# A fused hybrid decoder layer: two more groups of projections as Strassen's seven products, sums of x's blocks beside its normalisation, LayerNorm summed in the convolution

## The chip, the cores and the metric

The kernel runs on one core of one Trainium2 chip. The metric is the device time of one execution in microseconds. The kernel before takes 827.84 us, the median of 3 runs from 827.66 to 827.86.

The core has a matrix engine (TensorE, "PE" in the profile, with its weight loads apart as "PEld"), a vector engine (VectorE, "DVE"), a scalar engine (ScalarE, "ACT"), GpSimd ("POOL") and SyncE ("SP"), which here issues DMAs only. GpSimd and ScalarE issue a few DMAs too. Each engine takes its instructions in the order in which they were written into the program.

## The reference

x is one sequence of 512 tokens by 2048 channels, float32. The layer is:

```python
h = rms_norm(x, norm_g)
z = h @ w_in                                # 2048 x 7168
a_val, a_glu, a_gate, q, k, v, b_gate = jnp.split(z, SPLIT_POINTS, axis=-1)    # 1024 columns each
u = a_val * jax.nn.sigmoid(a_glu)
u = causal_depthwise_conv(u, conv_w, conv_b)                 # 31 taps
u = jax.nn.silu(layer_norm(u, conv_norm_g, conv_norm_b))     # over the 1024 channels of a token
u = u @ conv_pw_w + conv_pw_b                                # 1024 x 1024
y_a = u * jax.nn.silu(a_gate)
q, k = rms_norm of each of 16 heads
o = dilated_attention_mixture(q, k, v)
y_b = o * jax.nn.silu(b_gate)
return x + jnp.concatenate([y_a, y_b], axis=-1) @ w_out      # 2048 x 2048
```

## The kernel before

**Layout and exactness.** Everything stands transposed: channels on the 128 partitions, the 512 tokens along the free axis; x is 16 tiles of 128x512. Float32 products are made from halves: a number becomes a high half in float16 and a low half (the remainder) in float16, and `tri` (lines 366 to 368) multiplies high by high, high by low and low by high into the same bank of PSUM. So each product of a 128x128 block with 512 columns is three matmuls.

**Groups and units.** The weights are cut into groups of 512 output columns, in the order vg 0 to 3 (value and gate columns of the convolution branch together), q 0, k 0, v 0, bg 0, q 1, k 1, v 1, ag 0, ag 1, bg 1 (gates), pw 0, pw 1 (the pointwise projection, 1024 rows), wb 0 to 3 and wa 0 to 3 (the output projection in two parts). A unit is 4 k-blocks of a group: one load of 1 MB into a buffer `wf` (a ring of 6). vg 0 and vg 1, 8 units, run on raw x with another exact split (line 824). From vg 2 on a unit is 8 slots of 6 matmuls; a group of 16 k-blocks is 4 units, 192 matmuls of 512 columns. The weights of the next unit are split while the present one is multiplied: ScalarE makes the high half `wh` of 128x2048 (line 290), VectorE the low half `wl`, and then the buffer is free for the load of the unit six on. A float16 scale for each group comes from the sums of squares of its loaded weights (`measure`, line 182, four per group, then a small matmul, POOL and VectorE).

**The seven products.** The wa groups are already multiplied as 2x2 blocks by Strassen's scheme in Winograd's form: seven products of blocks instead of eight, with sums s1 to s4 of weight blocks and t1 to t4 of blocks of y. A part is a weight block of 128x1024 in two halves (`ws`, line 891 and the low beside it); its matmuls have 256 columns. The sums of weights are made in the load buffers, by DMAs of POOL's queue that accumulate, or by VectorE.

**Who orders the work.** There is no automatic scheduler. The program runs a clock of slots (`clock`); `after(n, fn)` puts a piece of work n slots later in a `calendar`; each slot first issues what is due, then `run_conv`, then the slot's 6 matmuls. `run_conv` fills VectorE with the convolution: each VectorE instruction is counted as 180 plus its free size (`Weighed`), a slot takes PACE = 1200 off the count, and convolution steps are issued while the count is below zero.

**The convolution and LayerNorm** (`conv`) are one generator. Each of 8 channel tiles takes 30 VectorE instructions on 128x512 (`cv<-u,cw,cv`) and one on ScalarE. Then LayerNorm: the 8 tiles are added into `lnacc`, a matmul with ones gives the mean (line 508), the tiles are centred and their squares added into `lnacc2`. `token_rsqrt` (line 344 on) takes the sum over channels with 4 small matmuls (line 350) into `lncol` (tokens on partitions), POOL takes the power -1/2 (line 160), four VectorE instructions make a diagonal, and a matmul with ones (line 360) spreads it to a row on all partitions, which ScalarE copies to `lnrow` (line 361). Each tile is multiplied by `lnrow` on VectorE, ScalarE applies Silu, and `split16` makes the two float16 halves of the tile `u` for the groups pw, both halves on VectorE. The projection's first unit is not written into the program before all 8 tiles are.

**Attention** runs in pairs of heads, 8 pairs, each beside 32 slots of projections: scores (line 663), maxima on VectorE, exponentials on ScalarE, halves `hl` of the normalised weights (for pairs 0 to 3 the high half on ScalarE, for pairs 4 to 7 on VectorE; the low half on VectorE), transposes by DMA, values (line 706).

```python
def run_conv():
    V.load = min(max(V.load - PACE, -PACE), 4 * PACE)
    wait[0] -= 1
    while (V.load < 0 or wait[1]) and wait[0] <= 0:
        n = next(convolution, 1)
        if n:
            wait[0] = n
```

## Time and profile before

| of the profiled execution | |
|---|---|
| its time, and its span | 827.54 us, 825.7 us |
| PE busy | 821.4 us, 99% |
| PEld busy | 458.9 us, 56% |
| DVE busy | 657.7 us, 80% |
| ACT busy | 502.4 us, 61% |
| POOL busy | 110.9 us, 13% |
| granted TensorE clock | 9 tenths of full speed or more in all 40 slices |
| PE waited for others | 1.2 us |
| DMA | 116.10 MB, mean 141 GB/s |

The span is the time from the first to the last instruction that the profiler saw; the execution's own time also has what lies around it. Busy time is the time in which an engine had an instruction running. [...] A row of a group reads: line, engine, operation, out<-in by the program's names, shapes, count, then busy us and mean ns of one, then the engine's idle time before it and what ended it. A row of a timeline reads: start, duration, engine, line, operation. The columns of the other views are told where they are shown.

### The profile page before, as it was taken

The numbers are of one execution on the slowest core, as the hardware profiler recorded it, in microseconds if no ns is written. First come the engines' busy times: TensorE is split into PE (matmuls) and PEld (weight loads), VectorE is DVE, ScalarE is ACT, GpSimd is POOL, SyncE is SP. The second block draws the span as 40 slices with busy tenths as digits, with TensorE's granted clock in tenths as the row PEclk, the third lists the DMA queues.
The fourth block names the chain that finished last, engine by engine and source line by source line (L and its number), as shares of the span: only waits on it lengthen the run. The fifth ranks groups of instructions, "written<-read, shape, count | busy, mean of one in ns | idle before, by whom it ended". The sixth has DMA issues, their size and how long they took to land.

```text
span 825.7 us, 12385 instructions
## 1 busy us (share of the span) xinstructions
PE 821.4 (99%) x4839; PEld 458.9 (56%) x4839; DVE 657.7 (80%) x1110; ACT 502.4 (61%) x683; POOL 110.9 (13%) x139
## 2 busy tenths in 40 slices
PE   9999999999999999999999999999999999999998
PEld 6887644444444444444444444444444444688887
DVE  6758889888888988878787978556765898988985
ACT  6666654353654446767674846766675758765741
POOL 0000010101413100002203101000010002413420
PEclk9999999999999999999999999999999999999999
DMA  9832232323344432626363753445252467579852
GB/s 334 331 123 102 102 105 100 109 95 108 110 128 124 136 111 103 165 103 165 84 177 93 184 132 106 135 109 159 86 132 103 136 207 252 106 176 266 160 100 67
DMA packets 88858, 116.10 MB, mean 141 GB/s; under 512 B 62176, under 2 KB 74208, under 8 KB 79584
## 3 DMA queue, kind: packets, MB, share of 16 engines
q1 hardware_dynamic: 80544, 107.37, 41.7%
q0 software_dynamic: 7968, 7.87, 6.7%
q8 instruction: 38, 0.62, 0.3%
q14 instruction: 20, 0.16, 0.1%
q10 hardware_dynamic: 288, 0.07, 0.0%
HBM read 88.56 MB, written 4.19 MB: 112 GB/s over the span
## 4 chain that ended last, share of the span: by engine, by line
PE 99%; DMA 0%; ACT 0%; DVE 0%; issue 0%; ACTq 0%
PE ps_l L366 26%; PE ps_l L368 26%; PE ps_l L367 26%; PE ps_l L824 11%; PE ps_s L367 2%; PE ps_s L366 2%; PE ps_s L368 2%; PE ps_s L663 2%; PE ps_o L706 2%; DMA wf<-w_dram 0%; PE ps_s L360 0%; PE ps_s L350 0%; PE ps_s L508 0%; ACT hh L322 0%; DVE res L72 0%; ACT wr L276 0%
## 5 line engine op out<-in xcount | busy, mean ns | idle before, releaser
L290 ACT ACTIVATE wh<-wf,ws 128x2048 f16<-128x2048 f32 x56 | 111.9, 1998 | 143.4 <-PE ps_l L367 137.4
L72 DVE SCALAR_TENSOR_TENSOR cv<-u,cw,cv 128x511 f32<-128x511 f32 (+14 forms) x240 | 160.9, 728 | 0.0
L72 DVE SCALAR_TENSOR_TENSOR wl<-wf,ws,wh 128x2048 f16<-128x2048 f32 x57 | 133.9, 2349 | 31.5 <-ACT wh L290 30.8
L366 PE MATMUL ps_l<-x,wh 128*128 128x512 f16 x384 | 145.6, 379 | 0.0
L366 PE MATMUL ps_l<-wh,x 128*128 128x512 f16 x384 | 145.6, 379 | 0.0
L368 PE MATMUL ps_l<-wh,x 128*128 128x512 f16 x384 | 145.5, 379 | 0.0
L367 PE MATMUL ps_l<-wl,x 128*128 128x512 f16 x384 | 145.5, 379 | 0.0
L368 PE MATMUL ps_l<-x,wl 128*128 128x512 f16 x384 | 145.5, 379 | 0.0
L367 PE MATMUL ps_l<-x,wh 128*128 128x512 f16 x384 | 145.5, 379 | 0.0
L182 ACT ACTIVATE junk<-wf 128x2048 bf16<-128x2048 f32 x68 | 129.1, 1899 | 2.4 <-DMA wf<-w_dram 2.1
L366 PEld LDWEIGHTS <-wh 128*128 128x128 f16 x544 | 53.2, 98 | 63.0 <-issue 3.9
L368 PEld LDWEIGHTS <-wl 128*128 128x128 f16 x544 | 53.2, 98 | 60.8
L367 PEld LDWEIGHTS <-wh 128*128 128x128 f16 x544 | 53.2, 98 | 58.1 <-issue 0.7
L196 POOL TENSOR_SCALAR ws<-ws 128x1 f32<-128x1 f32 x22 | 11.0, 499 | 401.3 <-DVE ws L72 401.3
L366 PEld LDWEIGHTS <-x 128*128 128x128 f16 x384 | 37.6, 98 | 46.5 <-issue 1.9
L368 PEld LDWEIGHTS <-x 128*128 128x128 f16 x384 | 37.6, 98 | 45.2
L367 PEld LDWEIGHTS <-x 128*128 128x128 f16 x384 | 37.6, 98 | 43.9
L891 ACT ACTIVATE ws<-wf,ws 128x1024 f16<-128x1024 f32 x28 | 32.0, 1144 | 29.3 <-DVE ws L72 6.3
L824 PE MATMUL ps_l<-xr,wr 128*128 128x512 f32 x192 | 48.2, 399 | 0.0
L824 PEld LDWEIGHTS ps_l<-xr,wr 128*128 128x128 f32 x192 | 36.1, 188 | 9.1 <-issue 0.5
L675 ACT ACTIVATE sx<-sx,st,sc 128x128 f32<-128x128 f32 (+1 forms) x64 | 40.9, 640 | 0.1
L72 DVE CUSTOM_DVE_ANT_0 sx<-ps_s,tab 128x512 f32<-128x512 f32 (+3 forms) x64 | 27.6, 487 | 16.5 <-PE ps_s L663 16.5
(213 smaller groups left out, 1394.6 us busy)
## 6 DMA issues: line engine op xcount, KB each, us to landing
wf<-w_dram SPq DMA_DIRECT2D x72, 1024.0 KB, 4.9
wf<-wf POOLq DMA_DIRECT2D x12, 512.0 KB, 5.9
x<-xt_dram SPq DMA_DIRECT2D x16, 256.0 KB, 6.9
res<-xt_dram SPq DMA_DIRECT2D x8, 512.0 KB, 6.8
out_dram<-res SPq DMA_DIRECT2D x15, 256.0 KB, 2.3
wf<-w_dram SPq DMA_DIRECT2D x7, 512.0 KB, 7.2
wf<-wf POOLq DMA_DIRECT2D x6, 256.0 KB, 6.2
wf<-w_dram SPq DMA_DIRECT2D x2, 256.0 KB, 3.3
```

Of the source, the lines that this page charges most:

```text
L72: return getattr(self.engine, name)(out, src, *args, **kw)
L182: A.activation(junk[:, :n], src, AF.Square, scale=scale, accum_out=acc)
L196: G.tensor_scalar(scale, scale, 1e-30, 2.0 ** (-2 * top), op0=OP.max, op1=OP.mult)
L290: A.activation(parts[i][0], raw[i], AF.Copy, scale=wscale[units[i][3:]][0])
L366: T.matmul(ps, ah, bh, start=first, stop=False)
L367: T.matmul(ps, ah, bl, start=False, stop=False)
L368: T.matmul(ps, al, bh, start=False, stop=last)
L663: T.matmul(ps[i, a], qs[hf, q][rows, p4, i * P:w], ks[hf, k][rows, p4, :w], start=n == 0, stop=n == 2)
L675: A.activation(xi, xi, AF.Exp, scale=sc, bias=neg[a][:, i:i + 1], accum_out=total[a][:, i:i + 1])
L706: T.matmul(po[rows, i * P:(i + 1) * P], vs[hf][j // 2][:, j % 2, 2 * p4 + a, vp * DH:(vp + 1) * DH], got["t", a][:, pp * (ALL // P) + FROM ...
L824: T.matmul(banks[group, m], wt[:, a, m * P:(m + 1) * P], xk[b], start=k == 0 and a == b == 0, stop=k == KC - 1 and a == 1)
L891: A.activation(t[:, 0], block(name), AF.Copy, scale=wscale["wa", g][0])
```

## The change

1. **vg 3 and v 0 as seven products.** A new function `input_products` does for these two groups what the wa groups do: 28 steps of 12 matmuls with 256 columns, 336 in a group. 14 parts of 128x1024 take the place of 4 splits of 128x2048. Each part's high half is on ScalarE, ordered 5 steps ahead of its matmuls, the low half on VectorE 4 steps ahead. Of the sums of weights, s2, s3 and s4 are accumulating DMAs of POOL's queue (two of each in a group), s1 is on VectorE. The products are combined on VectorE and ScalarE in tiles `cb`.
2. **Sums of x's blocks.** The right operands t1 to t4 are made for all 8 pairs of k-blocks by `sum_x`, from slot 58 on, one pair every 5 slots: four subtractions or additions on 128x256, two copies to float16 on ScalarE, two remainders on VectorE, into tiles `tx`. The normalised x (`xn`) is kept in slots for that.
3. **LayerNorm's sum** over the 8 tiles is made as the tiles are finished, all but the last two.
4. **LayerNorm's row** no longer goes through the diagonal and the matmul: POOL's queue writes `lncol` to memory (`by_token`) and reads it back spread over the partitions.
5. **Shorter order after it.** Waits for a given slot are dropped; product, Silu and split of a tile follow each 2 slots instead of 3; the first half in `split16`, and the high half of attention pairs 4 to 7, go from VectorE to ScalarE. The projection's units are written once the tiles they need are there, not all 8.
6. **Numbers.** The ring of load buffers has 8, `SLOTS` 35, PACE 1220, and 1400 from the first attention pair on. Two scale constants change. The DMA descriptor scratch of the queues is 2048 instead of the default. q's and k's normalisation is moved to a function (`norm_qk`) with the same work, for q and k as they stand.

Over the whole program VectorE has 24 more instructions with a scalar and two tensors, 64 more of two tensors and 48 fewer of a scalar and a tensor; ScalarE 87 more activations; POOL 14 more DMAs; TensorE 287 more matmuls, of which the two groups are 2 x (336 - 192) = 288.

```diff
-RING = 6
+RING = 8
-SLOTS = 36
+SLOTS = 35
-PACE = 1200
+PACE = 1220
-V_SHIFT = 16
-G_SHIFT = 10
+V_SHIFT = 13
+G_SHIFT = 8
...
+SEVEN = (("vg", 3), ("v", 0))
+LAST_SEVEN = SEVEN[-1]
+BY_DMA = ("s2", "s3", "s4")
+SUM_FROM = 58
+SUM_STEP = 10
+PACE_2 = 1400
+MEASURE = 8
...
-        V.tensor_scalar(t[:, 0, :], src, scale, None, op0=OP.mult)
+        A.activation(t[:, 0, :], src, AF.Copy, scale=scale)
...
-        t = temp("xn")
+        t = xn[k] = slot("xn")
...
+    def sum_x(j):
+        k = j + 4 * (j // 4)
+        (b11, b12), (b21, b22) = ((t[:, :H], t[:, H:]) for t in (xn.pop(k), xn.pop(k + 4)))
+        t12, t34 = temp("xs"), temp("xs")
+        t1, t2, t3, t4 = t12[:, :H], t12[:, H:], t34[:, :H], t34[:, H:]
+        to = tx[j] = (wide if j < 4 else att).tile([P, 4, 2, H], F16, name="tx", tag="wide" if j < 4 else "att")
+        V.tensor_sub(t1, b11, b12)
+        V.tensor_sub(t3, b12, b22)
+        V.tensor_add(t2, b22, t1)
+        V.tensor_sub(t4, b21, t2)
+        both = lambda t: t.rearrange("p (n t) -> p n t", n=2)
+        def high():
+            for n, t in ((0, t12), (2, t34)):
+                A.activation(to[:, n:n + 2, 0], both(t), AF.Copy)
+        def low():
+            for n, t in ((0, t12), (2, t34)):
+                V.tensor_tensor(to[:, n:n + 2, 1], both(t), to[:, n:n + 2, 0], op=OP.subtract)
+        after(1, high)
+        after(2, low)
...
+        if n == C:
+            by_token = dram.tile([S], F32, name="by_token")
+            G.dma_start(by_token.rearrange("(t p) -> p t", p=P), c)
+            G.dma_start(row, by_token.partition_broadcast(P))
+            return
...
+            if i0 == 0:
+                acc = slot("lnacc")
+                V.tensor_add(acc, cv[0], cv[1])
+            elif i0 < 6:
+                for i in (i0, i0 + 1):
+                    V.tensor_add(acc, acc, cv[i])
+                    yield 0
         wait[1] = True
-        acc = temp("lnacc")
-        V.tensor_add(acc, cv[0], cv[1])
-        yield 0
-        for i in range(2, 8):
+        for i in (6, 7):
             V.tensor_add(acc, acc, cv[i])
-            yield 1
         yield 3
...
-        while clock[0] % 8 != 4 or any(0 <= clock[0] - n < 8 for n in at_pair.values()):
+        while any(0 <= clock[0] - n < 8 for n in at_pair.values()):
             yield 1
         c = small.tile([P, NT], F32, name="lncol")
         row = temp("lnrow")
         for _ in token_rsqrt(acc2, C, LN_EPS, c, row):
-            yield 2
-        yield 2
+            pass
+        yield 7
         for i in range(8 + 2):
             if i < 8:
                 V.tensor_mul(cv[i], cv[i], row)
             if 1 <= i < 8 + 1:
                 A.activation(cv[i - 1], cv[i - 1], AF.Silu, scale=lng[:, i - 1:i], bias=lnb[:, i - 1:i])
-            yield 2
+            yield 1
             if i >= 2:
                 u16[i - 2] = split16(cv.pop(i - 2), scales["u"][0], "u16")
...
-            if hf == 0:
-                A.activation(hi, xi, AF.Copy, scale=r)
-            else:
-                V.tensor_scalar(hi, xi, r, None, op0=OP.mult)
+            A.activation(hi, xi, AF.Copy, scale=r)
...
-        V.load = min(max(V.load - PACE, -PACE), 4 * PACE)
+        pace = PACE_2 if 0 < min(at_pair.values(), default=0) <= clock[0] else PACE
+        V.load = min(max(V.load - pace, -pace), 4 * pace)
...
+    def input_products(i0):
+        kind, g = group = units[i0][3:]
+        by_token = kind in ("q", "k", "v")
+        weights, bank, got, done, free = {}, {}, {}, set(), set()
+        e = {}
+        def block(name, pair):
+            b = PLACE.get(name, name)
+            return raw[i0 + 2 * pair + (b[2] == "2")][:, :, H * (b[1] == "2"):][:, :, :H]
+        def add(name, pair):
+            if name == "s1":
+                V.tensor_tensor(block("a11", pair), block("a22", pair), block("a11", pair), op=OP.subtract)
+            else:
+                x, to = SUMS[name]
+                if name in BY_DMA:
+                    nc.gpsimd.dma_start(block(to, pair), block(x, pair), accum_op=OP.add)
+                else:
+                    V.tensor_tensor(block(to, pair), block(to, pair), block(x, pair), op=OP.add)
+        def hi(name, pair):
+            t = weights[name, pair] = part_pool.tile([P, 2, KU, H], F16, name="ws", tag="part")
+            A.activation(t[:, 0], block(name, pair), AF.Copy, scale=wscale[group][0])
+        def lo(name, pair):
+            t = weights[name, pair]
+            V.scalar_tensor_tensor(t[:, 1], block(name, pair), wscale[group][0], t[:, 0], op0=OP.mult, op1=OP.subtract)
+            done.add((name, pair))
+            for j in range(4):
+                mine = ("s2", "s4") if j % 2 else ("s1", "s3")
+                if all((n, j // 2) in done for n in mine) and all(m in free for m in range(j)) and j not in free:
+                    free.add(j)
+                    raw.pop(i0 + j)
+                    load(i0 + j + RING)
+                    after(MEASURE, lambda j=j: measure(i0 + j + RING))
...
+        ORDER = (("p1", "a11", "b11"), ("u", "a22", "t4"), ("x", "a12", "b21"), ("p7", "s3", "t3"), ("p5", "s1", "t1"),
+                 ("p6", "s2", "t2"), ("z", "s4", "b22"))
+        def product(n, pair, m):
+            to, w, x = ORDER[n]
+            if (pair, m) == (0, 0):
+                bank[to] = lin_ps.tile([P, 2, H], F32, name="ps_l", tag="ps_l")
+            ps, ms = bank[to][:, m], slice(m * P, (m + 1) * P)
+            for k in range(KU):
+                t, xs = weights[w, pair], x_part(x, pair, k)
+                first, last_ = pair == m == k == 0, pair == m == 1 and k == KU - 1
+                if by_token:
+                    tri(ps, [x[:, ms] for x in xs], (t[:, 0, k], t[:, 1, k]), first, last_)
+                else:
+                    tri(ps, [t[:, j, k, ms] for j in range(2)], xs, first, last_)
...
+        plan = [(2, scales_of), (4, lambda: copy("p1")), (8, lambda: copy("u")), (12, first_block), (16, lambda: copy("p7")),
+                (25, joint), (26, fifth), (27, sixth), (29, final), (30, lambda: out("12"))]
+        plan += [(26 if kind == "v" else 13, lambda: out("11")), (27, lambda: out("22")), (28, lambda: out("21"))]
+        if group == LAST_SEVEN:
+            plan.append((24, tx.clear))
+        plan += [(n, lambda name=name, pair=pair: add(name, pair)) for n, name, pair in
+                 ((-8, "s3", 0), (-7, "s3", 1), (3, "s2", 0), (4, "s2", 1), (8, "s4", 0), (9, "s4", 1), (9, "s1", 0), (11, "s1", 1))]
+        for n, (_, name, _) in enumerate(ORDER):
+            for pair in range(2):
+                at = 4 * n + 2 * pair - 5 + ((n, pair) == (1, 0))
+                plan += [(at, lambda name=name, pair=pair: hi(name, pair)), (at + 1, lambda name=name, pair=pair: lo(name, pair))]
+                for m in range(2):
+                    def matmuls(n=n, pair=pair, m=m):
+                        product(n, pair, m)
+                    plan.append((4 * n + 2 * pair + m, matmuls))
+        return plan
...
-            for k in range(KC):
-                after(NORM_FROM + k * (70 - NORM_FROM) // KC, lambda k=k: norm_x(k))
+            for n in range(KC):
+                after(NORM_FROM + n * (70 - NORM_FROM) // KC, lambda k=n // 2 + 4 * (n // 8) + 4 * (n % 2): norm_x(k))
+            for j in range(8):
+                after(SUM_FROM + SUM_STEP * j // 2, lambda j=j: sum_x(j))
...
-        if kind == "pw" and i == of_group[group][0]:
-            while 7 not in u16:
+        if kind == "pw":
+            need = KU * units[i][2] + KU - 1
+            while need not in u16:
...
-    nc = bacc.Bacc("TRN2", target_bir_lowering=False, num_devices=1)
+    nc = bacc.Bacc("TRN2", target_bir_lowering=False, num_devices=1, dynamic_dma_scratch_size=2048)
```

The order of instructions at three places. First TensorE's, where vg 3 begins (operands `x` are the halves of the normalised x, `wh`, `wl` the halves of a unit's weights, `ws` those of a part). Before:

```order
L368 LDWEIGHTS wl
L368 MATMUL ps_l<-x_948,wl 128x512
L366 LDWEIGHTS wh
L366 MATMUL ps_l<-x_975,wh 128x512
L367 LDWEIGHTS wh
L367 MATMUL ps_l<-x_975,wh 128x512
```

and with the change:

```order
L411 LDWEIGHTS wh
L411 MATMUL ps_l<-x_1021,wh 128x512
L412 LDWEIGHTS wh
L412 MATMUL ps_l<-x_1021,wh 128x512
L413 LDWEIGHTS wl
L413 MATMUL ps_l<-x_1021,wl 128x512
L411 LDWEIGHTS ws
L411 MATMUL ps_l<-x_638,ws 128x256
L412 LDWEIGHTS ws
L412 MATMUL ps_l<-x_638,ws 128x256
```

Each matmul still has a weight load of its own; the columns are 256 where they were 512.

Second POOL's, around LayerNorm's row (`lncol` is a value for each token, tokens on partitions; `ws` and `esc` are group scales). Before:

```order
L160 TENSOR_TENSOR lncol_4784<-lncol_4784,half_115 128x4
L196 TENSOR_SCALAR ws_4831<-ws_4831 128x1
L160 TENSOR_TENSOR ws_4831<-ws_4831,half_115 128x1
L379 TENSOR_TENSOR esc_4941<-wi_4412,xinv_127 128x1
L196 TENSOR_SCALAR ws_4992<-ws_4992 128x1
```

and with the change:

```order
L169 TENSOR_TENSOR lncol<-lncol,half 128x4
L396 DMA by_token<-lncol 128x4x1
L397 DMA lnrow<-by_token 128x512
L205 TENSOR_SCALAR ws<-ws 128x1
L169 TENSOR_TENSOR ws<-ws,half 128x1
```

The two DMAs stand behind the power and ahead of the next group's scale. On TensorE there are 132 matmuls of 512 columns between the column sums (L390 with the change) and the first matmul of pw 0; before, the timeline has them 72 us apart.

Third VectorE's, from the first product with `lnrow` to the first low half of `u` (`hl` are attention's halves, `wl` a unit's low half, `ws` and `wi` scales). Before:

```order
L72 TENSOR_TENSOR cv<-cv,lnrow 128x512
L72 SCALAR_TENSOR_TENSOR hl<-sx,st_4663,hl 128x128
L72 SCALAR_TENSOR_TENSOR hl<-sx,st_4663,hl 128x256
L72 SCALAR_TENSOR_TENSOR hl<-sx,st_4663,hl 128x384
L72 SCALAR_TENSOR_TENSOR hl<-sx,st_4663,hl 128x512
L72 TENSOR_SCALAR ws<-ws 128x1
L72 RECIPROCAL wi<-ws 128x1
L72 TENSOR_TENSOR cv<-cv,lnrow 128x512 x2
L72 SCALAR_TENSOR_TENSOR wl<-wf,ws,wh 128x2048
L72 TENSOR_SCALAR u_4947<-cv,us 128x512
L72 SCALAR_TENSOR_TENSOR u_4947<-cv,us,u_4947 128x512
```

and with the change:

```order
L80 TENSOR_TENSOR cv<-cv,lnrow 128x512
L80 SCALAR_TENSOR_TENSOR hl<-sx,st_5552,hl 128x128
L80 SCALAR_TENSOR_TENSOR hl<-sx,st_5552,hl 128x256
L80 SCALAR_TENSOR_TENSOR wl<-wf,ws,wh 128x2048
L80 SCALAR_TENSOR_TENSOR hl<-sx,st_5552,hl 128x384
L80 SCALAR_TENSOR_TENSOR hl<-sx,st_5552,hl 128x512
L80 TENSOR_SCALAR ws<-ws 128x1
L80 RECIPROCAL wi<-ws 128x1
L80 TENSOR_TENSOR cv<-cv,lnrow 128x512 x2
L80 SCALAR_TENSOR_TENSOR hl<-sx,st_5553,hl 128x128
L80 SCALAR_TENSOR_TENSOR hl<-sx,st_5553,hl 128x256
L80 SCALAR_TENSOR_TENSOR u_5805<-cv,us,u_5805 128x512
```

The first half of `u` (`u<-cv,us` in two operands) is gone from VectorE and the low half follows the second and third product directly; the fourth low half of `u` is 26 rows after the first product, with two low halves of units, 8 of attention, two gates and five small instructions among them. With the change the first unit of pw 0 is written once the first four tiles are.

193 lines of the change are left out of this document (158 added, 35 removed).

## The prediction

> **What bounds the kernel now.** I read the page first, then who TensorE waited for, then its order of time. The page's busy time and its chain of waits:
> ```profile
> PE 821.4 (99%) x4839; PEld 458.9 (56%) x4839; DVE 657.7 (80%) x1110; ACT 502.4 (61%) x683; POOL 110.9 (13%) x139
> PE 99%; DMA 0%; ACT 0%; DVE 0%; issue 0%; ACTq 0%
> ```
> The waits of engine PE, all of them:
> ```profile
> PE ps_s L138 <- POOL wz L135: 1.0, 1, 1.0
> PE ps_l L824 <- ACT hh L322: 0.2, 1, 0.2
> ```
> The numbers of a waits row are the us waited, how often, and the longest. TensorE waits 1.2 us in 825.7, at the start. So the time is the number of matmuls by the spacing of their starts, at a granted clock of 1.00 (rows below), and a change counts by the matmuls that it takes away and by the waits that it puts in. A matmul's duration says nothing of that (0.38 us for one of 512 columns, which starts 0.216 us after the last). The spacing is read from TensorE's timeline; both stretches hold 30 matmuls, so 29 spacings:
> ```profile
> 699.71 0.38 PE L368 MATMUL ps_l<-y,wl 128*128 128x512 f16 x1
> ...
> 705.97 0.38 PE L367 MATMUL ps_l<-y,wh 128*128 128x512 f16 x1
> 741.74 0.27 PE L366 MATMUL ps_l<-y,ws 128*128 128x256 f16 x1
> ...
> 744.91 0.27 PE L368 MATMUL ps_l<-y,ws 128*128 128x256 f16 x1
> ```
> 512 columns: 6.26/29 = 0.2159 us. 256 columns: 3.17/29 = 0.1093 us, in the wa groups, which already run seven products with a weight load for each matmul.
>
> **The change, part by part.**
>
> *Matmuls of vg 3 and v 0.* Each group goes from 192 of 512 columns to 336 of 256: 192 x 0.2159 = 41.45 us becomes 336 x 0.1093 = 36.72 us, 4.73 us less; twice, 9.46 us.
>
> *LayerNorm's spreading matmul.* The diagonal goes, and with it one piece of the chain of waits (second row; the first, the column sums, stays):
> ```profile
> 549.38 0.79 PE ps_s L350 x8
> 555.37 0.86 PE ps_s L360 x2
> ```
> 0.86 us less. **Saved: 10.32 us.** All else of the change only counts if TensorE has to wait for it.
>
> *Preparing the weights.* A group's 4 splits of 128x2048 become 14 of 128x1024, two sums on VectorE and six accumulating DMAs on POOL. Rows of the groups:
> ```profile
> L891 ACT ACTIVATE ws<-wf,ws 128x1024 f16<-128x1024 f32 x28 | 32.0, 1144 | 29.3 <-DVE ws L72 6.3
> L72 DVE SCALAR_TENSOR_TENSOR ws<-wf,ws 128x1024 f16<-128x1024 f32 x28 | 35.7, 1279 | 2.4 <-ACT ws L891 2.3
> wf<-wf POOLq DMA_DIRECT2D x12, 512.0 KB, 5.9
> ```
> A part is due 5 steps after its first half is ordered; a step is 12 matmuls, 1.31 us. 1.14 + 1.28 = 2.4 us against 6.6: hidden by 4 us. The s3 sum is ordered 15 steps (19.7 us) ahead of its use, s2 12 steps, s4 11: each against 5.9 us, hidden, even with 8 us for the second of a pair. The s1 sum waits on VectorE for the s2 DMA, 6 steps (7.9 us) after it: behind it stand lows and convolution, and it is 2 us early. POOL's queue behind a waiting DMA holds only group scales that are due a group later.
>
> *VectorE as a whole.* Added: 8 sums of x's blocks, each 4 subtractions of 256 and 2 of 512 (20 us in all, estimated from 0.60 us for one of 512, row below); a group's 14 lows for 4, its sums and its recombination, about 14 us each. Nearly all of it displaces convolution, which fills the steps. The filling is read here, in the stretch of vg 2 (PE, PEld, DVE, ACT and POOL busy, then clock and DMA) and in the timeline just after it:
> ```profile
> 97.00:138.50 41.50, 41.50 (x194) 18.80 (x193) 35.80 (x48) 20.79 (x21) 3.45 (x3) 1.00 0.31 110
> 141.17 2.34 DVE L72 SCALAR_TENSOR_TENSOR wl<-wf,ws,wh 128x2048 f16<-128x2048 f32 x1
> 143.43 7.15 DVE L72 SCALAR_TENSOR_TENSOR cv<-u,cw,cv 128x495 f32<-128x495 f32 x11
> 150.67 2.35 DVE L72 SCALAR_TENSOR_TENSOR wl<-wf,ws,wh 128x2048 f16<-128x2048 f32 x1
> ```
> One low and 11 taps are 2228 + 11 x 675 = 9650 units of the pacing, 8 x 1200, and took 9.4 us from low to low (141.17 to 150.67 is 9.50); a unit is 48 x 0.2159 = 10.4. At 1220 a step has 1.19 us of VectorE work in 1.30 (1.31 in seven products): still under. At 1400, once attention runs, it has 1.37 us. A step is longer there by the attention's own matmuls; from the first scores of one pair to those of the next, 32 steps:
> ```profile
> 306.84 0.61 PE L663 MATMUL ps_s<-k,q 64*128 64x512 f16 x4
> 352.16 0.82 PE L663 MATMUL ps_s<-k,q 64*128 64x512 f16 x5
> ```
> 45.32/32 = 1.42 us. It fits narrowly; a burst (the k group's evacuation ahead of v 0) can make a first part late by one low, 1.28 us. Three groups start behind such bursts: 0 to 3.8 us, and I take 1.0, for v 0 alone.
>
> *The convolution's end.* The 48 us of VectorE work (20 + 2 x 14) that come ahead of it, and the slack that they eat, are the point on which the sum hangs. Before, from the tile u (the halves that the pointwise projection reads) and in the LayerNorm stretch:
> ```profile
> L72 DVE SCALAR_TENSOR_TENSOR u<-cv,us,u x8: 720/752/752, 571.3 to 601.5; 128x512 f16<-128x512 f32 x8
> L366 PE MATMUL ps_l<-u,wh x64: 376/379/390, 622.2 to 666.9; 128*128 128x512 f16 x64
> ```
> The column sums end at 550.2, the projection starts 72 us later, and the last half was 20 us early. In the new order only 132 matmuls of 512 stand between: 28.5 us, 44 less. I work out when the fourth half (needed 6 matmuls later, at 29.8) is ready, from the column sums' end:
> ```profile
> 550.20 0.16 DVE L72 TENSOR_SCALAR lncol<-ps_s 128x4 f32<-128x4 f32 x1 [1.79 <-PE ps_s L350]
> 550.44 1.17 POOL L160 TENSOR_TENSOR lncol<-lncol,half 128x4 f32<-128x4 f32 x1 [35.97 <-DVE st L72]
> 558.87 2.34 DVE L72 SCALAR_TENSOR_TENSOR wl<-wf,ws,wh 128x2048 f16<-128x2048 f32 x1
> 561.13 0.68 DVE L72 TENSOR_TENSOR cv<-cv,lnrow 128x512 f32<-128x512 f32 x1
> 561.73 1.93 DVE L72 SCALAR_TENSOR_TENSOR hl<-sx,st,hl 128x128 f16<-128x128 f32 x4
> 563.58 0.14 DVE L72 TENSOR_SCALAR ws<-ws 128x1 int32<-128x1 int32 x1
> 571.25 0.75 DVE L72 SCALAR_TENSOR_TENSOR u<-cv,us,u 128x512 f16<-128x512 f32 x1
> 571.92 0.69 DVE L72 TENSOR_TENSOR cv<-cv,lnrow 128x512 f32<-128x512 f32 x1
> ```
> Root ready: 1.4. Then two DMAs on POOL, one after the other, and VectorE, with all queued behind it, waits for the second. No row shows them. Nearest rows:
> ```profile
> wf<-w_dram SPq DMA_DIRECT2D x72, 1024.0 KB, 4.9
> out_dram<-res SPq DMA_DIRECT2D x1, 64.0 KB, 1.6
> qg<-q_g_dram SPq DMA_DIRECT2D x1, 32.0 KB, 3.1
> wf<-wf POOLq DMA_DIRECT2D x6, 256.0 KB, 6.2
> ```
> Below: 1.6 out, 3.1 back (also a row spread over partitions), 4.7. Above: 6.2 each, and 3 more behind a 1 MB load (1024 KB by 4.9 us in the first of these rows; the load that the low ahead of lncol frees), 15.4. I take 10.5, near the POOL row. Then the rows of VectorE in the new order up to the fourth low, by start-to-start times above: 6 products by the row at 0.60, 8 attention lows at 1.85 for four, 2 weight lows at 2.26, 4 halves and 2 gates at 0.67, 5 small at 0.1: 3.6 + 3.7 + 4.5 + 4.0 + 0.5 = 16.3. Hand-overs to ACT and back (Silu, copy) at 5 places, 0.8 each: 4. Ready at 1.4 + 10.5 + 16.3 + 4 = 32.2; needed at 29.8: **2.4 us of waiting**, and 0.6 for the eighth half, one unit later. Ends: 26.4 (no wait) and 37.1 (7.3 us).
>
> [...]
>
> *At nothing:* splits moved from VectorE to ACT, which has 20 us free in the stretch from the column sums to the projection (fourth pair of numbers):
> ```profile
> 550.00:622.00 72.00, 72.00 (x404) 33.40 (x404) 48.65 (x107) 51.48 (x68) 5.81 (x11) 1.00 0.47 128
> ```
> Also at nothing: two more load buffers, the smaller descriptor scratch (three DMAs of 512 KB in flight at most), and the block sums of x, ordered in the stretch where VectorE is busy 68 of 92 us (if the last is late, vg 3 waits by the excess, 1 to 2 us):
> ```profile
> 5.00:97.00 92.00, 91.84 (x399) 73.39 (x399) 68.45 (x123) 63.34 (x104) 4.51 (x7) 1.00 0.56 209
> ```
>
> **Sum.** 825.7 - 10.3 + 1.0 + 3.0 = 819.4 us of span. The profiled execution ran 827.54, 1.84 around the span; the runs' median lies 0.30 above it: 819.4 + 1.84 + 0.30 = **821.5 us**.
>
> **Rivals.**
> *Nothing comes back* (0.17): the DMA pair takes 7 us or less, and bursts stay covered: 827.84 - 10.3 = 817.5. For it: the 1.6 and 3.1 us rows. Against: 3 us of slack where there were 20.
> *LayerNorm's path holds the projection* (0.12): the pair at 15 us, 7.3 of waiting, the three late starts at 3.8: 827.84 - 10.3 + 11.1 = 828.6 at the most, 825 in the middle. For it: POOL's rows of 6.2.
> *VectorE cannot feed the seven products* (0.10): a part's low comes later than its matmuls, part after part, since a group needs 14 x 1.28 + 2.6 + 5 = 25.5 us of VectorE work in 36.7 us before any tap. It decides if taps ahead in the queue take more than the remaining 11 us, 15 taps. With half of the added 28 us exposed: 827.84 - 10.3 + 14 = 831.5, slower. Against: the pacing counts the lows.
> *The change doesn't do what it says* (0.03): the spacing of 256-column matmuls rises with these operands; at 41.45/336 = 0.123 us nothing is saved: 827. Against: the wa rows above are the same form.
> [...]
>
> **How the numbers follow.** Forecast 0.58. A measurement can tell 0.2%, 1.7 us. Faster: forecast, nothing back, and two thirds of the second rival: 0.83. Same (the fourth rival and a quarter of the second) 0.06, slower (the third rival and the top of the second) 0.11. Range 817 to 828: the first rival's time, and the upper ends of the two waits; the starved case is left out.
>
> **What would show it.** Right: matmuls of 256 columns 0.109 us apart in vg 3 and v 0; PE's waits a few us, at the projection's first units, on VectorE's or ACT's u; lnrow's DMA landing about 10 us after the root; VectorE busier before LayerNorm. Wrong: PE waiting inside the seven products, on ws lows or on accumulated wf; waits over 8 us at the projection; or waits in attention, where VectorE was given 1400 a step.

## The result, and the profile after

The changed kernel takes 833.31 us, the median of 4 runs from 832.02 to 835.92, against 827.75 us for the kernel before beside it (827.59 to 827.86): a ratio of 1.0073, 95% interval 1.0061 to 1.0085. It is 0.7% slower, where 821.5 us, faster, had been forecast. Its profiled execution has a span of 830.6 us where the working gave 819.4, so 11.2 us are to be found.

Busy time and the chain of waits, from the page of the changed kernel:

```profile
PE 815.7 (98%) x5125; PEld 488.0 (59%) x5125; DVE 690.4 (83%) x1150; ACT 547.0 (66%) x768; POOL 124.2 (15%) x154
PE 82%; DVE 5%; DMA 5%; issue 3%; ACT 2%; POOL 2%; SPq 0%; POOLq 0%; ACTq 0%; DVEq 0%
```

TensorE is no longer the whole chain. Whom it waited for, the main rows of its waits (us, how often, the longest):

```profile
PE ps_l L411 <- ACT u L312: 2.6, 1, 2.6
PE ps_l L413 <- DVE wl L80: 1.9, 2, 1.1
PE ps_l L413 <- DVE ws L80: 1.7, 2, 0.9
PE ps_l L412 <- DVE ws L80: 1.6, 3, 0.8
...
PE ps_l L411 <- ACT ws L1125: 0.8, 1, 0.8
```

These rows undercount, because a matmul's 0.27 or 0.38 us of busy time covers the beginning of the wait behind it. The spacing of the starts tells all of it. TensorE's timeline at five places of the changed kernel:

```profile
174.73 0.27 PE L412 MATMUL ps_l<-x,ws 128*128 128x256 f16 x1
175.93 0.28 PE L413 MATMUL ps_l<-x,ws 128*128 128x256 f16 x1 [0.93 <-DVE ws L80]
...
178.34 0.38 PE L411 MATMUL ps_l<-wh,x 128*128 128x512 f16 x1
180.15 0.38 PE L412 MATMUL ps_l<-wl,x 128*128 128x512 f16 x1 [1.43 <-DVE wl L80]
...
301.91 0.38 PE L412 MATMUL ps_l<-x,wh 128*128 128x512 f16 x1
303.40 0.39 PE L413 MATMUL ps_l<-x,wl 128*128 128x512 f16 x1 [1.11 <-DVE wl L80]
...
621.37 0.38 PE L412 MATMUL ps_l<-u,wh 128*128 128x512 f16 x1
622.50 0.39 PE L413 MATMUL ps_l<-u,wl 128*128 128x512 f16 x1 [0.76 <-DVE ws L80]
...
623.95 0.38 PE L413 MATMUL ps_l<-u,wl 128*128 128x512 f16 x1
626.92 0.38 PE L411 MATMUL ps_l<-u,wh 128*128 128x512 f16 x1 [2.60 <-ACT u L312]
```

Each spacing less its regular 0.1093 or 0.2159 us is a stall: 1.09 us at the end of vg 3, 1.59 at the unit behind it, 1.27 at the unit behind v 0, 0.92 and 2.75 at the projection's first unit. All places taken together, in the same way: 2.0 us inside vg 3, 1.6 behind it, 2.1 inside v 0, 1.3 behind it, 5.5 from 610 us to the projection's eighth half, and about 1 before and at the start of vg 2. That is 13.5 us against 10.3 saved. The clock adds to it. In the row of the stretch 620 to 640 us (PE, PEld, DVE, ACT, POOL busy, then the granted clock) it is 0.91, and in the chain of waits attention's 58 value matmuls behind the last stall take 3.32 us where the same step takes 1.80 for 60 elsewhere:

```profile
620.00:640.00 20.00, 16.24 (x134) 8.42 (x132) 14.80 (x29) 16.06 (x24) 0.94 (x3) 0.91 0.41 104
```
```profile
349.27 1.80 PE ps_o L760 x60
...
628.36 3.32 PE ps_o L760 x58
```

So 825.7 - 10.3 + 13.5 + 1.5 = 830.4, the span to 0.2 us. The question is why each stall is there.

**POOL's queue.** The issues of the accumulating DMAs of vg 3, from POOL's timeline of the changed kernel:

```profile
145.27 1.34 POOL L1119 DMA_DIRECT2D wf<-wf  x1 [0.33 <-issue]
151.08 1.31 POOL L1119 DMA_DIRECT2D wf<-wf  x1 [4.47 <-DMA wf<-wf]
157.26 1.29 POOL L1119 DMA_DIRECT2D wf<-wf  x1 [4.86 <-DMA wf<-wf]
163.34 1.31 POOL L1119 DMA_DIRECT2D wf<-wf  x1 [4.79 <-DVE cv L80]
```

The second sum works on another pair of units and needs nothing of the first, but is issued only when the first has landed, 5.8 us later; so do the third and fourth. The fourth lands at 173.3, 10.0 us after its issue, where the three before it took 5.5 to 5.9. In those 10 us the DMA engines moved 287 GB/s, and 95, 92 and 124 while the three before it were under way, by the view of busy time by stretches. ScalarE's timeline shows who stands behind it:

```profile
173.41 1.15 ACT L1125 ACTIVATE ws<-wf,ws 128x1024 f16<-128x1024 f32 x1 [4.55 <-DMA wf<-wf]
174.46 1.99 ACT L300 ACTIVATE wh<-wf,ws 128x2048 f16<-128x2048 f32 x1
```

The last part's first half waits 4.55 us for that sum, and the first half of q 0's first unit stands behind it. That is the stall inside vg 3 and the one after it.

**LayerNorm's row.** The chain of waits from the power to the first product:

```profile
592.98 1.02 POOL lncol L169
...
594.37 8.55 DMA by_token<-lncol
...
603.49 4.00 DMA lnrow<-by_token
...
607.51 0.69 DVE cv L80
```

13.5 us from the power's end to VectorE's first product, of which the way out, 2 KB, takes 8.6. Its packets in the trace, 16 of 128 bytes, all start between 596.5 and 597.3; what fills the 5.6 us from there to the landing is not shown.

### The profile page after: what moved, and what is told of

Its sections match the earlier page's. It is cut to its first block, busy times and chain, and to the rows that moved or that the text cites. A ratio compares the mean times of both kernels' runs of the same rounds, so it can differ in the third digit from the quotient of the medians.

```text
span 830.6 us, 13114 instructions
## 1 busy us (share of the span) xinstructions
PE 815.7 (98%) x5125; PEld 488.0 (59%) x5125; DVE 690.4 (83%) x1150; ACT 547.0 (66%) x768; POOL 124.2 (15%) x154
## 4 chain that ended last, share of the span: by engine, by line
PE 82%; DVE 5%; DMA 5%; issue 3%; ACT 2%; POOL 2%; SPq 0%; POOLq 0%; ACTq 0%; DVEq 0%
PE ps_l L411 21%; PE ps_l L413 21%; PE ps_l L412 21%; PE ps_l L876 10%; DMA wf<-wf 4%; PE ps_o L760 2%; PE ps_s L413 2%; PE ps_s L411 2%; PE ps_s L412 2%; PE ps_s L720 2%; DVE ws L80 1%; DVE wl L80 1%; DMA by_token<-lncol 1%; DVE cv L80 1%; ACT junk L191 1%
## 5 line engine op out<-in xcount | busy, mean ns | idle before, releaser
L300 ACT ACTIVATE wh<-wf,ws 128x2048 f16<-128x2048 f32 x48 | 95.8, 1995 | 72.1 <-PE ps_l L412 72.1
L80 DVE SCALAR_TENSOR_TENSOR wl<-wf,ws,wh 128x2048 f16<-128x2048 f32 x49 | 115.1, 2348 | 13.4 <-ACT wh L300 13.3
L413 PE MATMUL ps_l<-x,wl 128*128 128x512 f16 x320 | 121.4, 379 | 1.9 <-DVE wl L80 1.9
L412 PE MATMUL ps_l<-wl,x 128*128 128x512 f16 x320 | 121.3, 379 | 1.4 <-DVE wl L80 1.4
L411 PE MATMUL ps_l<-x,wh 128*128 128x512 f16 x320 | 121.4, 379 | 0.3 <-DVE glu L80 0.3
L411 PE MATMUL ps_l<-wh,x 128*128 128x512 f16 x320 | 121.4, 379 | 0.0
L413 PE MATMUL ps_l<-wh,x 128*128 128x512 f16 x320 | 121.3, 379 | 0.0
L412 PE MATMUL ps_l<-x,wh 128*128 128x512 f16 x320 | 121.3, 379 | 0.0
L80 DVE SCALAR_TENSOR_TENSOR ws<-wf,ws 128x1024 f16<-128x1024 f32 x56 | 71.4, 1278 | 11.9 <-ACT ws L1125 9.9
L876 PE MATMUL ps_l<-xr,wr 128*128 128x512 f32 x288 | 70.7, 401 | 0.1
L876 PEld LDWEIGHTS ps_l<-xr,wr 128*128 128x128 f32 x288 | 54.6, 190 | 14.4 <-ACT xr L336 1.0
L80 DVE TENSOR_TENSOR wr<-wf,wr 128x512 fp32r<-128x512 f32 x32 | 22.1, 691 | 24.0 <-ACT wr L286 23.9
```

The costliest lines, as they stand in the source:

```text
L80: return getattr(self.engine, name)(out, src, *args, **kw)
L300: A.activation(parts[i][0], raw[i], AF.Copy, scale=wscale[units[i][3:]][0])
L411: T.matmul(ps, ah, bh, start=first, stop=False)
L412: T.matmul(ps, ah, bl, start=False, stop=False)
L413: T.matmul(ps, al, bh, start=False, stop=last)
L876: T.matmul(banks[group, m], wt[:, a, m * P:(m + 1) * P], xk[b], start=k == 0 and a == b == 0, stop=k == KC - 1 and a == 1)
```

## The experiments

All times are medians; ratios are to the kernel before, run beside it.

**1 and 2. The descriptor scratch, with a ring of 7.** To leave room for a scratch of 8192 both runs have 7 load buffers, and the first is the control.

```diff
-RING = 8
+RING = 7
-MEASURE = 8
+MEASURE = 5
```
```diff
-    ... dynamic_dma_scratch_size=2048)
+    ... dynamic_dma_scratch_size=8192)      # the second run only
```

> Control for the next run: the changed kernel with a ring of 7 load buffers instead of 8 (the measurement of a unit's weights is put 5 slots after its load instead of 8, so that the scale of q 0 is there in time); descriptor scratch 2048 as in the change. Both theories expect the same here: the six accumulating DMAs of a group still follow one another at 6.2 us (151.08 to 157.26 in the changed kernel), TensorE still stands in vg 3 and v 0, 832 to 836 us against 833.3.

> The control with a descriptor scratch of 8192 instead of 2048. Theory A (the small scratch lets POOL's queue hold one 512 KB DMA at a time: POOL's second s2 instruction starts when the first DMA has landed, 151.08 against a start of 145.27 and 5.9 us to landing, though the two are of different pairs): the second s2 starts within 2.5 us of the first, the last s4 lands some 6 us earlier, the stalls inside vg 3 and v 0 (about 7 us by the spacing of the matmul starts) shrink to under 2 us, 826 to 829 us. Theory B (the DMAs are slow because weight loads take the DMA engines, 93% busy from 160 to 180 us): POOL issues closer together but each DMA lands later by as much, the stalls stay, 832 us or more.

The control took 845.62 us (1.0218, 1.0203 to 1.0234), the larger scratch 843.07 (1.0188, 1.0171 to 1.0204). The control alone costs 12 us, which nobody had expected: a measurement on ScalarE now stands ahead of q 0's first half and waits for its load.

```profile
175.47 1.91 ACT L191 ACTIVATE junk<-wf 128x2048 bf16<-128x2048 f32 x1 [0.89 <-DMA wf<-w_dram]
...
177.39 1.99 ACT L300 ACTIVATE wh<-wf,ws 128x2048 f16<-128x2048 f32 x1
```

So the ring of 8 (or the later measurement, which had to change with it) is part of what keeps the seven products fed. POOL's timeline with the larger scratch shows what theory A expects: both s2 sums are issued in one go, within 2.7 us, where the control shows 142.77 and 148.55:

```profile
142.32 2.66 POOL L1119 DMA_DIRECT2D wf<-wf  x2 [17.34 <-DVE ws L80]
```

2.5 us came back, less than expected. The loads now set the end of each group: ScalarE waits 4.7 us for one at 174.1 and 5.3 us at 305.2, each time just ahead of the next unit's first half. Run 5 is the cleaner test.

**3. LayerNorm's row by the matmul.**

```diff
-        if n == C:
-            by_token = dram.tile([S], F32, name="by_token")
-            G.dma_start(by_token.rearrange("(t p) -> p t", p=P), c)
-            G.dma_start(row, by_token.partition_broadcast(P))
-            return
...
-            pass
-        yield 7
+            yield 2
+        yield 2
```

> The changed kernel with LayerNorm's row made as before (diagonal on VectorE, matmul with ones, ScalarE's copy) instead of the two DMAs through memory; the ring of 8 and the scratch of 2048 stay. Theory: the two DMAs are what holds the projection (8.6 us out and 4.0 back after the power, 13.5 in all; the forecast took 10.5). The row then comes some 5 us after the power instead of 13.5, TensorE's stalls at pw 0's first unit (about 5 us) go, the granted clock does not fall to 0.91 from 620 to 640 us, and 0.9 us of matmul comes back: 826 to 828 us. Rival (VectorE's and ScalarE's work between the row and the halves is what holds, not the row): less than 2 us gained, 831 to 833 us.

826.52 us, 0.9990 (0.9981 to 0.9999): 6.8 us less than the changed kernel, as expected. TensorE no longer waits on any u, and the granted clock is 1.00 from 620 to 640 us. In this run it falls elsewhere, to half from 177.0 to 180.4, behind the stalls of 1.0 and 1.1 us in vg 3. The stretch 160 to 180 us, which has 1.00 in the changed kernel:

```profile
160.00:180.00 20.00, 18.19 (x151) 15.09 (x150) 16.03 (x19) 12.72 (x12) 1.30 (x1) 0.93 0.92 256
```

It costs next to nothing there, because TensorE has to wait for q 0's first low half until 180.1 in both kernels.

**4. Both, with the ring of 7.**

> Ring of 7, scratch of 8192 and LayerNorm's row by the matmul together. If theory A and the theory on LayerNorm both hold, the gains add: 833.3 less 5 less 6.5, about 820 to 823 us, which would be faster than the kernel before (827.8). If one of them falls, 826 to 829; if both, 831 or more.

837.82 us (1.0121, 1.0104 to 1.0137). The ring of 7 spoils it: against its own control, 843.07, the matmul gains 5.3. It says nothing on the sum of the two cures.

**5. The scratch alone, with the ring of 8,** on top of run 3. Two measurements of 128x1024 in place of one of 128x2048 make the room.

```diff
-    junk = const.tile([P, KU * S], BF16, name="junk")
+    junk = const.tile([P, KU * S // 2], BF16, name="junk")
...
-            row_squares(raw[i].rearrange("p k n -> p (k n)"), sums[group][:, j:j + 1], KU * S)
+            for n in range(2):
+                row_squares(raw[i][:, 2 * n:2 * n + 2]..., sums[group][:, 2 * j + n:2 * j + n + 1], KU * S // 2)
...
-    ... dynamic_dma_scratch_size=2048)
+    ... dynamic_dma_scratch_size=4096)
```

> On top of LayerNorm's row by the matmul (826.5), with the ring at 8: the scratch is 4096 instead of 2048. The room for it comes from measuring each unit's weights in two halves of 128x1024 instead of one of 128x2048, which gives ScalarE some 0.2 us more per unit. Theory A: two DMAs of 512 KB are in flight at a time, the last sum lands some 6 us earlier, 822 to 825 us. Theory B (DMA engines are what is short): nothing, 826 to 828 us.

823.18 us, 0.9948 (0.9933 to 0.9963): 3.3 us from the scratch, although ScalarE has more to do. POOL's timeline in vg 3:

```profile
145.41 2.68 POOL L1115 DMA_DIRECT2D wf<-wf  x2 [0.27 <-issue]
151.72 1.29 POOL L1115 DMA_DIRECT2D wf<-wf  x1 [3.63 <-DMA wf<-wf]
155.05 1.28 POOL L1115 DMA_DIRECT2D wf<-wf  x1 [2.04 <-DMA wf<-wf]
```

The fourth sum is issued at 155.05 instead of 163.34 (163.44 in run 3), and takes 6.5 us to land instead of 10.0. So of the 11.8 us by which it lands earlier than in the changed kernel, 8.3 are the queue's and 3.5 the landing's. Theory A holds at vg 3; theory B, the slow landing beside loads, falls as the only cause but has a share.

By the spacing of the starts, the stalls in and behind vg 3 fall from 3.9 us in run 3 to 0.9. In and behind v 0 they do not: 2.9 us before and 3.4 now, though the fourth sum there is issued 10 us earlier too. What holds there is ScalarE's queue, in which the last parts' first halves stand behind a measurement that waits for its load. ScalarE's and VectorE's timelines of this run:

```profile
288.82 1.06 ACT L191 ACTIVATE junk<-wf 128x1024 bf16<-128x1024 f32 x1 [3.18 <-DMA wf<-w_dram]
...
292.23 1.28 DVE L80 SCALAR_TENSOR_TENSOR ws<-wf,ws 128x1024 f16<-128x1024 f32 x1 [3.83 <-ACT ws L1121]
```

**6. One sum fewer in the queue,** on top of run 3: the second s4 on VectorE, scratch 2048.

```diff
-                if name in BY_DMA:
+                if name in BY_DMA and (name, pair) != ("s4", 1):
...
-    (9, "s4", 1)
+    (14, "s4", 1)
```

> On top of LayerNorm's row by the matmul (826.5): the second s4 sum of each of the two groups is made by VectorE, at step 14, instead of by the fourth DMA of POOL's queue; ring 8 and scratch 2048 stay. Theory A (the queue of DMAs, one after the other, makes the last sum late; the fourth lands at 173.3, 5.8 us after its part is due at 140 + 21 x 1.31 = 167.5): the stalls at the end of vg 3 and v 0, and at the units behind them whose halves stand in the same queues (together some 5 us of matmul spacing), shrink to 1 or 2, 822 to 824 us. Rival (VectorE as a whole is too full there, and 1.2 us more in it moves the stall elsewhere): 826 to 828 us.

823.86 us, 0.9957 (0.9940 to 0.9973). A quite different cure of the same lateness brings 2.7 us, though it gives VectorE work, and again at vg 3 alone (3.9 us of stalls become 0.7; in and behind v 0 it is 3.1). The rival, a full VectorE, falls here.

**7. The row through memory in the kernel before.** The same five lines that run 3 takes out, with their waits, added to the kernel before.

> The kernel before with only one part of the change: LayerNorm's row through memory instead of through the diagonal and the matmul. Before, the last half of u came 20 us ahead of its matmuls. Theory (the DMA pair costs the changed kernel time only because other work ahead of it ate that slack): the pair takes 13 to 14 us here too, TensorE does not wait for it, and the time is 826.5 to 827.8 us (0.86 us of matmul gone). Rival (the pair hurts by itself, by what it holds up on VectorE's queue behind it): over 829 us, with waits of TensorE on wl lows in the 550s and 560s.

826.85 us, 0.9990 (0.9981 to 0.9999). The pair is slower than in the changed kernel (8.7 out, 7.3 back, from the DMA issues, where that has 8.6 and 4.0), VectorE waits for it, and TensorE does not wait for VectorE:

```profile
568.54 1.90 DVE L72 TENSOR_TENSOR cv<-cv,lnrow 128x512 f32<-128x512 f32 x3 [5.18 <-DMA lnrow<-by_token]
```
```profile
by_token<-lncol POOLq DMA_DIRECT2D x1, 2.0 KB, 8.7
lnrow<-by_token POOLq DMA_DIRECT2D x1, 256.0 KB, 7.3
```

It gains 0.9 us, the size of the diagonal's matmul. The pair costs time only where the slack is gone.

**8 and 9. No seven products,** with the row through memory and then by the matmul. Both compute vg 3 and v 0 as plain groups.

```diff
-SEVEN = (("vg", 3), ("v", 0))
-LAST_SEVEN = SEVEN[-1]
+SEVEN = ()
+LAST_SEVEN = None
```

> The changed kernel with vg 3 and v 0 as plain groups (no seven products, no weight sums, none of the 14 parts; the sums of x's blocks are still made); row through memory, ring 8, scratch 2048. The 9.5 us of matmuls are not saved. Theory (vg 3 and v 0 cost about 7 us of their own in stalls and 28 us of VectorE work, which makes LayerNorm late): the stalls in both groups are gone, LayerNorm's column sums end some 20 us earlier against the matmuls, the projection does not wait: 827 to 829 us. Rival (the other parts, the pacing and the sums of x, are what makes LayerNorm late): the projection still waits 3 us or more, 831 us or more.

> The run without seven products once more (834.1, one stall of 3.9 us in the 520s behind which the clock fell: a wl low stood behind the product that waited 9.0 us for lnrow's DMA), now with LayerNorm's row by the matmul. Theory (VectorE's queue, stopped by the DMA pair, is all that was lost there): no stall, 0.9 us of matmul back, 827.5 to 828.5 us. Rival (the other parts of the change cost something themselves): 830 us or more.

834.06 us (1.0074, 1.0059 to 1.0090) and 832.08 (1.0048, 1.0031 to 1.0064). Both expectations of mine were wrong. LayerNorm is early in these runs, the projection does not wait, and yet 4 to 6 us are lost at one place. VectorE's timeline without seven products, row through memory (run 8):

```profile
521.91 0.69 DVE L80 TENSOR_TENSOR cv<-cv,lnrow 128x512 f32<-128x512 f32 x1 [9.00 <-DMA lnrow<-by_token]
...
523.17 2.34 DVE L80 SCALAR_TENSOR_TENSOR wl<-wf,ws,wh 128x2048 f16<-128x2048 f32 x1
```

VectorE stands 9.0 us for lnrow, and a unit's low half stands behind it in the queue: TensorE waited 3.7 us on that `wl`. With the matmul instead (run 9), TensorE's timeline:

```profile
508.40 0.38 PE L408 MATMUL ps_l<-x,wl 128*128 128x512 f16 x1
510.80 1.12 PE L400 MATMUL ps_s<-diag,ones 128*128 128x512 f32 x2 [2.02 <-DVE diag L80]
...
512.08 0.63 PE L407 MATMUL ps_l<-x,wh 128*128 128x512 f16 x1
512.51 0.63 PE L408 MATMUL ps_l<-x,wl 128*128 128x512 f16 x1
...
515.39 0.38 PE L406 MATMUL ps_l<-x,wh 128*128 128x512 f16 x1
```

Here TensorE stands 2.2 us for the diagonal, and the matmuls behind it run at 0.43 us instead of 0.216 until 515.4. The diagonal was late because VectorE had waited 5.3 us for ScalarE's first half of y, with lncol behind it (run 8 has the same wait). ScalarE's and VectorE's timelines of run 9:

```profile
500.02 2.00 ACT L300 ACTIVATE wh<-wf,ws 128x2048 f16<-128x2048 f32 x1 [6.05 <-PE ps_l L407]
...
505.22 0.75 DVE L80 SCALAR_TENSOR_TENSOR y<-gate,yb0s,y 128x512 f16<-128x512 f32 x1 [5.33 <-ACT y L312]
...
508.15 0.15 DVE L80 TENSOR_SCALAR lncol<-ps_s 128x4 f32<-128x4 f32 x1
```

The half was not late for want of free time on ScalarE. ScalarE had stood idle for 6.05 us before `wh`, which had to wait for TensorE; behind `wh` stood four exponentials, and the half behind those (504.48). That half is one of those that the change moved to ScalarE. The runs 10 to 12 test that.

**10, 11 and 12. The first halves on VectorE again,** in the changed kernel, in run 9, and in the best order (runs 13 to 15).

```diff
     t = slots.tile([P, 2, S], F16, name=name, tag="slot")
-    A.activation(t[:, 0, :], src, AF.Copy, scale=scale)
+    V.tensor_scalar(t[:, 0, :], src, scale, None, op0=OP.mult)
```

> The changed kernel with one part undone: the first half of each 512-column tile of u and of y (the helper that splits them) is made on VectorE again instead of on ScalarE. The forecast put that part at nothing. Theory C (it is part of what made the projection late: the fourth u's first half stood on ScalarE behind other work, 626.26, and TensorE waited 2.6 us on it): the projection's stalls shrink by 2 us or more, the clock keeps its full rate there, 829 to 831 us. Theory D (the row through memory alone sets it): 832.5 us or more.

> The run without seven products and with the row by the matmul (832.1; there VectorE waited 5.3 us for ScalarE's first half of a y tile at 505, with the wl low, lncol and the diagonal behind it, and TensorE 2.2 us for the diagonal), now with the first halves on VectorE. Theory C: VectorE's wait and TensorE's stall go, 827.5 to 828.5 us, that is the kernel before's time. Rival (other parts of the change): 830 us or more.

> The best order so far (row by the matmul, scratch 4096, second s4 sum on VectorE, borders' halves earlier: 820.6), with the first halves on VectorE. VectorE gets 16 instructions of 0.48 us more. If ScalarE's queue still costs something there, 819.5 to 820.4; if VectorE's 7.7 us count, 821 to 823.

829.29 us (1.0019, 1.0009 to 1.0028), 828.66 (1.0011, 1.0001 to 1.0020) and 820.13 (0.9905, 0.9890 to 0.9920). The move costs the changed kernel 4.0 us by the medians: undone, TensorE's longest wait on `u` falls from 2.6 to 1.1 us, the stalls from 610 us on from 5.5 to 4.2 (2 us less had been expected), and in the profiled execution the clock stays whole (1.000 in the mean against 0.997). The clock seems to be the larger part. It is 0.998 or less in all four runs of the changed kernel and in three of the ten without the move; between the runs at 0.998 (one with the move, 832.0 us, three without, 830.3 to 830.5) the difference is only 1.5 to 1.8 us. Without seven products the move is most of what was left, as TensorE's waits in run 11 show:

```profile
PE ps_s L147 <- POOL wz L144: 1.0, 1, 1.0
PE ps_l L871 <- ACT xr L336: 0.6, 1, 0.6
PE ps_l L406 <- DVE glu L80: 0.3, 1, 0.3
```

No stall is left after 110 us. The other parts of the change (sums of x, the pacing) then cost 1.0 us against the kernel before, and the time lies just above the 827.5 to 828.5 expected; the trace has 0.6 us of it at vg 2's first units, behind a late glu.

**13, 14 and 15. What is left.** Run 5 with the second s4 on VectorE (13); run 5 with work at the groups' borders earlier in the queues (14); both (15).

```diff
-                    plan = [(24, lambda: split_hi(n_next)), (25, lambda: split_lo(n_next))] + plan
+                    plan = [(22, lambda: split_hi(n_next)), (24, lambda: split_lo(n_next))] + plan
...
-                at = 4 * n + 2 * pair - 5 + ((n, pair) == (1, 0))
+                at = 4 * n + 2 * pair - 5 + ((n, pair) == (1, 0)) - 2 * (n == 0)
```

> LayerNorm's row by the matmul, scratch 4096, and the second s4 sum on VectorE. If both were cures of the same lateness (the last sum of weights), the second adds nothing to 823.2: 822.5 to 823.7. If they were separate, 820 to 821.

> LayerNorm's row by the matmul, scratch 4096, and two things earlier in VectorE's and ScalarE's queues: the first part of a group by 2 steps, and the halves of the plain unit behind a group by 2 and 1 steps. Theory (what is left are late lows at the groups' borders: 0.9 us at q 0, 1.1 at v 0, 1.1 at bg 0 by the spacing of the matmul starts): 820 to 821.5 us. Rival (VectorE is full there, so the lateness moves to other parts): 822.5 to 824 us.

> All of them: LayerNorm's row by the matmul, scratch 4096, the second s4 sum on VectorE, the borders' halves earlier. 819.5 to 821.5 us by the theory that the stalls left are the borders' alone; 822.5 or more if VectorE is full.

821.66 us (0.9929, 0.9914 to 0.9944), 820.57 (0.9915, 0.9901 to 0.9930) and 820.65 (0.9914, 0.9900 to 0.9929). The two cures of the sums' lateness add 1.5 us to each other, between what the two theories said. The borders bring 2.6, as expected; with all of it together (run 15) no stall is left in vg 3 and 0.6 us in v 0. Run 12 is run 15 with the first halves on VectorE, and has the lowest time, 820.13 us; its interval overlaps that of run 15, so that the last 0.5 us are not shown. Its busy time and all of TensorE's waits:

```profile
PE 813.1 (99%) x5127; PEld 487.6 (60%) x5127; DVE 698.4 (85%) x1168; ACT 560.3 (68%) x893; POOL 125.8 (15%) x150
```
```profile
PE ps_s L147 <- POOL wz L144: 1.0, 1, 1.0
PE ps_l L408 <- DVE ws L80: 0.4, 1, 0.4
PE ps_l L407 <- DVE glu L80: 0.2, 1, 0.2
```

It beats the kernel before by 7.5 us, of the 9.5 that the matmuls give, with VectorE at 85% where the slower changed kernel has 83.

## Why the prediction was wrong

**What it got right.** The matmuls: outside the stalls their starts are 0.11 us apart in vg 3 and v 0, and 7.5 us of the gain remain in the best run. The diagonal: 0.86 forecast, 0.9 measured in run 7. An early part of v 0 late behind the k group's evacuation: 1.0 taken, 0.8 measured (268.1). VectorE's rows and the hand-overs from the first product to the fourth low half of u: 16.3 + 4 = 20.3 us forecast, 20.2 measured (607.5 to 627.7). That the slack ahead of the projection is what the sum hangs on: run 7 shows the same DMA pair at no cost where the slack is there.

**"Also at nothing: two more load buffers, the smaller descriptor scratch (three DMAs of 512 KB in flight at most)".** This failed first, for the scratch. I counted DMAs and did not ask how many are under way together with the smaller scratch. With 2048 each sum of vg 3 was issued only when the one before had landed, 5.8 to 6.2 us after it, where with 4096 the first two went out within 2.7 us; and "hidden, even with 8 us for the second of a pair" was worked out for two side by side; the fourth alone took 10.0. The s1 sum was not "2 us early" either: VectorE stood 3.6 and 2.8 us for the second s2 (at 156.97 and 282.03). Together with the borders' queues behind them it is the 7.0 us of stalls, 3.6 in and behind vg 3 and 3.4 in and behind v 0, where 1.0 was forecast. On top of run 3, the scratch is worth 3.3 us and one sum fewer 2.7, both at vg 3. The stalls of v 0 need more: they are 1.8 us with both cures (run 13) and 0.6 with the borders' work earlier too (run 15).

**"At nothing: splits moved from VectorE to ACT, which has 20 us free in the stretch".** The second failure, 4.0 us in run 10 and 3.4 in run 11. A share of busy time was taken for room in a queue. ScalarE's free time does not lie where the half is due: the half stands behind exponentials, measurements and gates, or behind a weight half that itself waits for TensorE, and VectorE's whole queue stands behind the half. In run 10 most of the 4.0 seems to be the clock, and some may be chance: the path from the first product to the fourth low half took 19.7 us for 20.2, but the row's way through memory, which the move does not touch, also 12.8 for 13.5. The 4.0 and the 6.8 of run 3 are two cures of the same stall and do not add.

**The DMA pair.** 10.5 us were taken within 4.7 to 15.4; it took 13.5 from the power to the first product. The sum lies in the bounds, but the way out does not: 8.6 us for 2 KB that the program writes as 512 single elements, where I had bounded one DMA by 1.6 and 6.2 from rows of larger transfers. The way out took 7.9 to 8.9 us in all six runs that have it. The root, too, was ready 2.3 us after the column sums (591.7 to 594.0) instead of 1.4, behind a unit's low half on VectorE (590.25 to 592.60) and a scale of another group on POOL. These two terms, 3.0 and 0.9 us too small, are all of the fourth half's lateness.

**The end of it.** The fourth low half of u was forecast for 32.2 us after the column sums; it was there at 627.7, 36.0 after them. "2.4 us of waiting and 0.6" became 5.5: 3.3 for the fourth half, 1.9 for two units' low halves that stood in VectorE's queue behind the product and were late as well (0.95 us at 610, 0.92 at 621), and 0.3 in small ones. Behind these stalls the clock fell to half (0.50 in the row of the stretch 628.1 to 631.5), for which the sum had no term: 1.5 us more.

**The rivals.** By its time the outcome is the third rival's, 831.5. Its mechanism was not: run 6 gives VectorE more to do and is faster, run 12 more again and is not slower. The sign that had been named for it did come, TensorE waiting inside the seven products on low halves (2.5 us in four of the waits above), but behind late sums, first halves and one evacuation, not part after part. What comes nearest in kind is the second, LayerNorm's path holding the projection, with the first group of stalls added to it. The two were priced apart, each with the other at its middle value; that they could come together, and with the clock, was left out of the range.

## What to carry to other kernels

Ask of each resource that a change makes smaller how many of the things in use are still under way together, not whether one gets through (here the second sum of vg 3 was issued 5.8 us after the first, where with the larger scratch two went out within 2.7). Price moved work by its place in the new engine's queue and by who stands behind the instruction that waits for it; a busy share of 70% says nothing of either. Slack that covers a slow path in one kernel can be spent by another part of the same change, so the path has to be priced again after that part.

## What the runs showed of the hardware

- In vg 3 the accumulating DMAs of 512 KB on POOL's queue were issued 5.8 to 6.2 us after one another with a descriptor scratch of 2048 (145.27, 151.08, 157.26, 163.34), and two of them within 2.7 us with 4096 or 8192 (runs 5 and 2). With 2048 one took 5.5 to 5.9 us to land where the DMA engines moved 92 to 124 GB/s, and 10.0 where they moved 287.
- A DMA to memory of 2 KB, written as 512 single elements, took 7.9 to 8.9 us, longer than the median of the 512 KB sums on the same queue (5.9).
- After TensorE had stood for 2.2 us (510.8, run 9), matmuls of 512 columns started 0.43 us apart, half the rate, until 515.4. Half the rate came also after 2.8 us (the changed kernel, granted clock 0.50 from 628.1 to 631.5) and 3.9 us (run 8), and in run 3 after two stalls of only 1.0 and 1.1 us, 2.5 us from first to last; the half rate lasted 3.4 us in each of these four. It did not come after 1.7, 1.1 and 1.6 us at the same place within 7.5 us in run 10 (172.8 to 180.1, granted clock 1.00). So the length of a stall alone does not decide it, and what does is not shown.
